# Decay matrices of a bidirectional state space layer: 512-column row matmuls and masks on the diagonal blocks only

## The chip, the cores and the metric

The kernel runs on one core of a Trainium2 chip. The time is the device time of one launch in microseconds (us), the median of several runs. Five engines work from instruction streams of their own: TensorE (PE, with its weight loads shown apart as PEld), VectorE (DVE), ScalarE (ACT), GpSimd (POOL) and SyncE (SP), which here issues the transfers. Matrix products land in PSUM, which has eight banks of 512 float32 columns on each of 128 partitions.

## What is computed

One layer of an encoder with 256 tokens and 1024 features: a gated feed-forward half step, a mixer that adds latent attention (16 heads) and a state space part (SSD), and a second half step. The change concerns the SSD part, which runs once forward and once backward over the tokens and has 32 heads in 4 groups of 8:

```
a_cs = cumsum(dt * a)                              # log decay up to each token
seg  = a_cs[l] - a_cs[s]
decay = exp(where(tril, seg, -inf))                # [l, s], per head
cb   = C @ B.T                                     # [l, s], per group
y    = (cb * decay) @ (x * dt)                     # plus the chunk states
y_total = y_forward + reverse(y_backward of reversed inputs)
```

The kernel does not scan chunks. It works on the full 256 x 256 matrix of token pairs, as 2 x 2 blocks of 128 x 128: the forward direction needs the two diagonal blocks (each a triangle) and one block beside them, the backward direction the two diagonal blocks (the other triangle) and the opposite one. Six blocks are needed for a head.

## The kernel before

Weights are float32. Each one that comes from memory is split by `wload` into a rounded part (`whi`, ScalarE, L94) and the rest (`wlo`, VectorE, L97), and every product with a weight is three matmuls of 256 columns in the type fp32r (`mm3`, L136 to L138). The first half step runs 22 blocks of such products and 8 for the way back; the second does the same at the end. Between them is the mixer.

In the mixer, `in_group` projects and convolves the inputs of one SSD group, `attn_group` does two attention heads, `ssd_group` one group of eight SSD heads as `start`, four times `pair`, and `finish`. These units, the gates' projections and half of the branch products are put into one list, `plan`, sorted by hand-set keys (`A0`, `DA`, `S0`, ...), and traced in that order. The build's scheduler then orders each engine's stream: it takes the ready instruction of the highest priority, where priority is the place in the trace, and where the splitting of weights is put ahead by 50 (`WPRI`). So matmuls of a projection may stand between those of a `pair`. Each engine then runs its stream in order.

For SSD, partition is the token `s` that gives and column the token `l` that takes. `tables` and the code from L463 prepare:

- `acs` [128, 2, 64], the sums of log decays, counted from the middle of the sequence outwards; `nacs` is its negative. Index 1 is the half of the sequence, index 2 the head (0 to 31 forward, 32 to 63 backward).
- `st1` and `st2` (L477 to L493), 256 columns each: the sums with heads on partitions and tokens on columns, as a rounded part and, on other partitions, a rest. `st1` holds forward and backward heads, `st2` for each half of the tokens the heads of the opposite direction.
- `sel1` and `sel2`, columns with a one at the partitions of a head. A column spread over 128 columns as the stationary operand gives a matmul that copies a head's row of `st1` or `st2` to all partitions.
- `msk`, three windows of `msk4` of 256 columns each: 0 where a pair of tokens counts and -2**100 elsewhere. With the identity `eye` as the stationary operand a matmul adds it.

`pair` takes two heads. It fills three PSUM banks `ps_pl` in turn, `i` = 0, 1, 2, each with 256 columns for either head: `i` = 0 is what the first half of the tokens gives going forward, `i` = 1 what the second half gives going backward, `i` = 2 the two diagonal blocks of the opposite directions. For each bank and head there is one matmul with the mask (L672) and one with the row (L673). ScalarE takes the exponential with `nacs` as bias (L678: 256 columns; L680 and L681: 128 each), VectorE multiplies the bank's 512 columns by `cb` (L683, shown as L97), and eight matmuls per pair (L690; float32, for which the profile shows two records each) sum the blocks into `ps_y`, in the order of the banks. There are two `ps_pl` buffers (`NPL`) and four `E` buffers (`EB`).

Of the kernel before, what the change touches and what calls it, by code (L numbers as in the profile page):

```python
# [8 lines left out]
F32 = mybir.dt.float32  # L9
F32R = mybir.dt.float32r  # L10
# [13 lines left out]
# pool depths  # L24
# [48 lines left out]
def build(ctx, tc, A, out, dbg=None):  # L73
# [131 lines left out]
    class Norm:  # L205
        """x * gain of each tile of x as it comes, and the sum of squares"""
# [159 lines left out]
    with ExitStack() as es:  # L366
# [63 lines left out]
        # rotated shared key and its square sum  # L430
# [12 lines left out]
        # dt = softplus(raw + bias), log-decay sums  # L443
# [22 lines left out]
        # log-decay sums counted from the middle of the sequence outwards  # L466
# [13 lines left out]
        for c in range(2):  # L480
            V.tensor_copy(dup[:, 0, c].rearrange("p (a b) -> p a b", a=2),
                          acs[:, c].unsqueeze(1).to_broadcast([P, 2, 64]))
            o = 32 * (1 - c)
            V.tensor_copy(dup[:, 1, c].rearrange("p (a b) -> p a b", a=4),
                          acs[:, c, o:o + 32].unsqueeze(1).to_broadcast([P, 4, 32]))
        pd = gbank("ps_dup")
        for i in range(2):
            for c in range(2):
                TE.transpose(pd[:, (2 * i + c) * P:(2 * i + c + 1) * P], dup[:, i, c], ident)
# [49 lines left out]
        def attn_group(g):  # L539
            st = {}  # L540

            def proj():
# [20 lines left out]
                # head norms  # L563
# [11 lines left out]
                # rotary part of q, in place  # L575
# [7 lines left out]
                # k  # L583
# [55 lines left out]
        def ssd_group(g, xz):  # L639
            st = {}  # L640

            def start():
# [6 lines left out]
                cb = (cb[:, 0:2], cb[:, 2:4], cb[:, 0:4:3])  # L649
                st["cb"] = cb  # L650
# [12 lines left out]
            def pair(p):  # L663
                cb = st["cb"]
                M = []
                for i in range(3):
                    pp = ps_pl.tile([P, 2, T], F32, tag="pl", name="ps_pl")
                    E = ss.tile([P, 2, T], F32, tag="E", name="E", bufs=EB)
                    for j in range(2):
                        h = 8 * g + 2 * p + j  # L670
                        lh = sel1[:, 32 * i + h:32 * i + h + 1] if i < 2 else sel2[:, h:h + 1]
                        TE.matmul(pp[:, j], eye, msk[i], start=True, stop=False)  # L672
                        TE.matmul(pp[:, j], lh.to_broadcast([P, P]), st1 if i < 2 else st2, start=False, stop=True)  # L673
                    for j in range(2):
                        h = 8 * g + 2 * p + j
                        if i < 2:
                            o = 32 * i + h
                            ends[1] = S.activation(E[:, j], pp[:, j], AF.Exp, bias=nacs[:, i, o:o + 1])  # L678
                        else:
                            S.activation(E[:, j, 0:P], pp[:, j, 0:P], AF.Exp, bias=nacs[:, 0, 32 + h:33 + h])  # L680
                            ends[1] = S.activation(E[:, j, P:T], pp[:, j, P:T], AF.Exp, bias=nacs[:, 1, h:h + 1])  # L681
                    E4 = E.rearrange("p j (a b) -> p j a b", a=2)
                    tt(E4, E4, cb[i].unsqueeze(1).to_broadcast([P, 2, 2, P]), ALU.mult)  # L683
                    M.append(E)
                py = gbank("ps_y")
                plan = ((0, 0, 0, 0, T), (1, 1, 1, 0, T), (0, 1, 2, 0, P), (1, 0, 2, P, T))
                for n, (c, d, i, a, b) in enumerate(plan):
                    for j in range(2):
                        hh_ = 2 * p + j
                        TE.matmul(py[64 * j:64 * j + 64, a:b], st[c, d][:, hh_], M[i][:, j, a:b],  # L690
                                  start=n == 0, stop=n == 3)
                y = st["y"][:, p]
                dc = V_DSK + 4 * g + p
                stt(y, xz[1 + p // 2][:, p % 2], vec[:, dc:dc + 1], py[:, :T], ALU.mult, ALU.add)
                tt(y, y, xz[3 + p // 2][:, p % 2], ALU.mult)

            def finish():
                y = st["y"]
                sq = [ss.tile([P, 2, T], F32, tag="E", name="ysq", bufs=EB) for _ in range(2)]
# [95 lines left out]
def _tiles(w):  # L795
    """[K, M] -> [M tiles, partition, K tiles, 128]"""
# [4 lines left out]
def _pairs(t):  # L801
    """[n, P, K, 128] -> [n / 2, P, 2 * K * 128]"""
# [89 lines left out]
```

## Time and profile before

| | us |
|---|---|
| median of 3 runs | 820.86 |
| lowest, highest | 820.34, 820.87 |
| profiled execution, from the first to the last instruction | 817.6 |
| PE idle in the span | 817.6 - 797.8 = 19.8 |

No other time is given for the profiled execution than its span; the median of the runs is 3.26 us above it.

The first half step lies at about 0 to 211 us, the mixer at 211 to 633, the second half step after that. The 16 calls of `pair` lie between 260.9 us, where the first matmul of `ps_pl` starts, and 555.4 us, where the last of `ps_y` does.

A matmul's length in the profile is its latency. Matmuls follow each other faster than that, so the distance from one start to the next says what one costs. In a row of a group the last part is the idle time of the engine just before these instructions, and what ended it; in a row of the timeline this stands in brackets.

### The profile page before, as it was taken

To read this page: it belongs to the slowest core of one execution; us is meant where nothing else is said; L and a number is where in the kernel's file an instruction comes from. 1 tells how busy PE (TensorE), PEld (TensorE's weight loads), DVE (VectorE), ACT (ScalarE), POOL (GpSimd) and SP (SyncE) were. 2 spreads that over 40 slices of the span, in tenths; PEclk is the share of its full clock that TensorE was granted. 3 is DMA by queue.
4 is the path that set the end of the run, shared out by engine and by line. 5 is a ranking of instruction groups with operands and counts; after the bars stand their busy time and mean duration, and the time that the engine had idled before them with its cause. 6 is when DMAs were issued, how large, how long until landed. Compare 5 with 4: busy or idle time off the path is not lost.

```text
span 817.6 us, 16082 instructions
## 1 busy us (share of the span) xinstructions
PE 797.8 (98%) x6480; PEld 768.8 (94%) x6480; DVE 590.3 (72%) x1192; ACT 470.2 (58%) x810; POOL 0.2 (0%) x4
## 2 busy tenths in 40 slices
PE   6999999999998999999999999999999999999998
PEld 5999999999998998988989999999999999999998
DVE  6977776566797986897897578657787766666543
ACT  6755554455367659679676666557455544444342
POOL 0000000000000000000000000000000000000000
PEclk9999999999999999999999999999999999999999
DMA  7667774667235443322325414342665555554772
GB/s 259 214 212 224 222 229 136 184 184 215 63 92 171 131 131 104 106 79 92 103 85 168 154 52 154 112 146 68 223 184 178 175 184 182 185 184 131 197 206 75
DMA packets 39098, 126.61 MB, mean 155 GB/s; under 512 B 4464, under 2 KB 5872, under 8 KB 39024
## 3 DMA queue, kind: packets, MB, share of 16 engines
q1 hardware_dynamic: 38592, 124.69, 48.7%
q8 instruction: 51, 0.84, 0.4%
q10 hardware_dynamic: 432, 0.89, 0.3%
q14 instruction: 23, 0.19, 0.1%
HBM read 124.52 MB, written 1.05 MB: 154 GB/s over the span
## 4 chain that ended last, share of the span: by engine, by line
PE 86%; DVE 6%; ACT 5%; DMA 2%; issue 1%; ACTq 0%
PE ps_gu L137 10%; PE ps_gu L138 10%; PE ps_gu L136 10%; PE ps_d L136 5%; PE ps_d L137 5%; PE ps_d L138 5%; PE ps_in L137 4%; PE ps_in L138 4%; PE ps_in L136 4%; PE ps_y L690 3%; PE ps_sb L138 2%; PE ps_sb L137 2%; PE ps_sb L136 2%; PE ps_sc L603 2%; PE ps_gt L137 1%; PE ps_o L630 1%
## 5 line engine op out<-in xcount | busy, mean ns | idle before, releaser
L94 ACT ACTIVATE whi<-raw 128x1024 fp32r<-128x1024 f32 (+4 forms) x256 | 251.3, 986 | 209.0 <-PE ps_d L137 53.1
L97 DVE TENSOR_TENSOR wlo<-raw,whi 128x1024 fp32r<-128x1024 f32 (+4 forms) x256 | 289.8, 1134 | 112.1 <-ACT whi L94 111.2
L136 PE MATMUL ps_gu<-xh,whi 128*128 128x256 f32 x704 | 201.0, 285 | 7.9 <-ACT whi L94 7.9
L137 PE MATMUL ps_gu<-xl,whi 128*128 128x256 f32 x704 | 201.2, 286 | 0.5 <-DVE xl L100 0.4
L138 PE MATMUL ps_gu<-xh,wlo 128*128 128x256 f32 x704 | 200.8, 285 | 0.0
L136 PEld LDWEIGHTS ps_gu<-xh,whi 128*128 128x128 f32 x704 | 136.5, 194 | 8.2 <-ACT whi L94 8.2
L137 PEld LDWEIGHTS ps_gu<-xl,whi 128*128 128x128 f32 x704 | 136.5, 194 | 1.0 <-DVE xl L100 0.9
L138 PEld LDWEIGHTS ps_gu<-xh,wlo 128*128 128x128 f32 x704 | 136.4, 194 | 0.5 <-DVE wlo L97 0.5
L137 PE MATMUL ps_in<-xl,whi 128*128 128x256 f32 x368 | 105.3, 286 | 0.1
L138 PE MATMUL ps_in<-xh,wlo 128*128 128x256 f32 x368 | 105.0, 285 | 0.0
L136 PE MATMUL ps_in<-xh,whi 128*128 128x256 f32 x368 | 104.4, 284 | 0.0
L137 PE MATMUL ps_d<-hl,whi 128*128 128x256 f32 x352 | 99.1, 281 | 0.0
L136 PE MATMUL ps_d<-hh,whi 128*128 128x256 f32 x352 | 99.1, 281 | 0.0
L138 PE MATMUL ps_d<-hh,wlo 128*128 128x256 f32 x352 | 99.0, 281 | 0.0
L137 PEld LDWEIGHTS ps_in<-xl,whi 128*128 128x128 f32 x368 | 70.1, 191 | 0.6 <-DVE xl L100 0.3
L138 PEld LDWEIGHTS ps_in<-xh,wlo 128*128 128x128 f32 x368 | 70.1, 191 | 0.5 <-issue 0.3
L136 PEld LDWEIGHTS ps_in<-xh,whi 128*128 128x128 f32 x368 | 70.1, 191 | 0.1
L136 PEld LDWEIGHTS ps_d<-hh,whi 128*128 128x128 f32 x352 | 66.3, 188 | 0.0
L137 PEld LDWEIGHTS ps_d<-hl,whi 128*128 128x128 f32 x352 | 66.3, 188 | 0.0
L138 PEld LDWEIGHTS ps_d<-hh,wlo 128*128 128x128 f32 x352 | 66.3, 188 | 0.0
L100 DVE SCALAR_TENSOR_TENSOR xz<-ps_in,vec,xz 128x254 f32<-128x254 f32 (+1 forms) x96 | 44.8, 476 | 1.6 <-ACT xz L520 0.9
L94 ACT ACTIVATE hh<-sg 128x256 fp32r<-128x256 f32 x44 | 18.1, 415 | 45.9 <-DVE sg L97 45.9
(222 smaller groups left out, 1467.5 us busy)
## 6 DMA issues: line engine op xcount, KB each, us to landing
raw<-in_w_gu SPq DMA_DIRECT2D x86, 512.0 KB, 4.5
raw<-in_w_in SPq DMA_DIRECT2D x62, 512.0 KB, 4.4
raw<-in_w_d SPq DMA_DIRECT2D x32, 384.0 KB, 3.2
raw<-in_w_d SPq DMA_DIRECT2D x32, 320.0 KB, 3.4
raw<-in_w_sb SPq DMA_DIRECT2D x16, 512.0 KB, 4.4
raw<-in_w_qkv SPq DMA_DIRECT2D x8, 544.0 KB, 3.8
raw<-in_w_ab SPq DMA_DIRECT2D x8, 512.0 KB, 3.8
raw<-in_w_o SPq DMA_DIRECT2D x8, 512.0 KB, 4.2
```

Source lines behind the costliest of these rows:

```text
L94: S.activation(dst, src, AF.Copy, scale=scale)
L97: V.tensor_tensor(out=dst, in0=a, in1=b, op=op)
L100: V.scalar_tensor_tensor(out=dst, in0=a, scalar=s, in1=b, op0=op0, op1=op1)
L136: TE.matmul(ps, whi, xhi, start=first, stop=False)
L137: TE.matmul(ps, whi, xlo, start=False, stop=False)
L138: TE.matmul(ps, wlo, xhi, start=False, stop=last)
L603: TE.matmul(sc[:, t * T:(t + 1) * T], qk[:HD, t * P:(t + 1) * P], qk[:HD, T:2 * T], start=True, stop=True)
L630: TE.matmul(po[64 * j:64 * j + 64, :T], kv[:, kt, HG * NOPE + hh_ * 64:HG * NOPE + (hh_ + 1) * 64], st[hh_][:, kt], start=kt == 0, stop=kt ...
L690: TE.matmul(py[64 * j:64 * j + 64, a:b], st[c, d][:, hh_], M[i][:, j, a:b], start=n == 0, stop=n == 3)
```

## The change

For each head one whole bank now holds forward (columns 0 to 255, given by the first half of the tokens) and backward (256 to 511, given by the second half). One matmul of 512 columns writes both rows from a wider `st1` [128, 2, 256], and one matmul of 256 columns adds the masks to the two diagonal blocks, columns 0 to 127 and 384 to 511; the other blocks get no mask. The third bank holds the opposite diagonal blocks of both heads: a matmul of 512 columns writes the masks (two blocks, repeated for the second head), two of 256 columns add the rows from `st2`. The exponentials keep their shapes and numbers. The product with `cb` on a head's bank is flat over 512 columns. `ps_y` takes the third bank first, then the two heads' banks. `sel1` and one mask block go; one `sel` of 32 columns serves forward and backward. The rest of the diff takes out comments.

```diff
-    sel1 = cp.tile([P, 64], F32R, name="sel1")
-    sel2 = cp.tile([P, 32], F32R, name="sel2")
+    sel = cp.tile([P, 32], F32R, name="sel")
     eye = cp.tile([P, P], F32R, name="eye")
-    msk4 = cp.tile([P, 4, P], F32R, name="msk4")
-    msk = (msk4[:, 2:4], msk4[:, 0:2], msk4[:, 1:3])
+    msk = cp.tile([P, 3, P], F32R, name="msk")
...
-        V.tensor_copy(sel1, cst[:, C_S1:C_S1 + 64])
-        V.tensor_copy(sel2, cst[:, C_S2:C_S2 + 32])
+        V.tensor_copy(sel, cst[:, C_S2:C_S2 + 32])
...
-        ts(msk4[:, 0], ones, 1.0, 2.0 ** 100, ALU.subtract, ALU.mult)
-        ts(msk4[:, 1], triB, 1.0, 2.0 ** 100, ALU.subtract, ALU.mult)
-        ts(msk4[:, 2], triF, 1.0, 2.0 ** 100, ALU.subtract, ALU.mult)
-        ts(msk4[:, 3], ones, 1.0, 2.0 ** 100, ALU.subtract, ALU.mult)
+        for i, tri in enumerate((triF, triB, triF)):
+            ts(msk[:, i], tri, 1.0, 2.0 ** 100, ALU.subtract, ALU.mult)
...
-        st1 = mp.tile([P, T], F32R, name="st1")
-        st2 = mp.tile([P, T], F32R, name="st2")
+        st1 = mp.tile([P, 2, T], F32R, name="st1")
+        st2 = mp.tile([P, 2, P], F32R, name="st2")
...
-        copy(st1, pd[:, 0:T])
-        tt(st1[64:128], pd[64:128, 0:T], st1[64:128], ALU.subtract)
-        copy(st2, pd[:, T:2 * T])
-        tt(st2[32:64], pd[32:64, T:2 * T], st2[32:64], ALU.subtract)
+        pd = pd.rearrange("p (a b) -> p a b", a=2)
+        copy(st1, pd)
+        tt(st1[32:64], pd[32:64], st1[32:64], ALU.subtract)
+        V.tensor_copy(st2[:, 0], st1[:, 1, 0:P].bitcast(F32))
+        V.tensor_copy(st2[:, 1], st1[:, 0, P:T].bitcast(F32))
...
             def pair(p):
                 cb = st["cb"]
+                h0 = 8 * g + 2 * p
+
+                def line(h):
+                    return sel[:, h:h + 1].to_broadcast([P, P])
+
+                def bank():
+                    return ps_pl.tile([P, 2, T], F32, tag="pl", name="ps_pl")
+
+                def decays(E, pieces, c):
+                    for a, b, src, k, o in pieces:
+                        ends[1] = S.activation(E[:, a:b], src, AF.Exp, bias=nacs[:, k, o:o + 1])
+                    tt(E, E, c, ALU.mult)
+
                 M = []
-                for i in range(3):
-                    pp = ps_pl.tile([P, 2, T], F32, tag="pl", name="ps_pl")
-                    E = ss.tile([P, 2, T], F32, tag="E", name="E", bufs=EB)
+                for j in range(2):
+                    h = h0 + j
+                    pp = bank()
+                    TE.matmul(pp, line(h), st1, start=True, stop=False)
+                    TE.matmul(pp.rearrange("p a (b c) -> p (a b) c", b=2)[:, 0:4:3], eye, msk[:, 0:2], start=False, stop=True)
+                    E = ss.tile([P, 2 * T], F32, tag="E", name="E", bufs=EB)
+                    decays(E, ((0, T, pp[:, 0], 0, h), (T, 2 * T, pp[:, 1], 1, 32 + h)), cb)
+                    M.append(E)
+
+                pp = bank()
+                TE.matmul(pp.rearrange("p a (b c) -> p a b c", b=2), eye,
+                          msk[:, 1:3].unsqueeze(1).to_broadcast([P, 2, 2, P]), start=True, stop=False)
+                for j in range(2):
+                    TE.matmul(pp[:, j], line(h0 + j), st2, start=False, stop=j == 1)
+                E = ss.tile([P, 2 * T], F32, tag="E", name="E", bufs=EB)
+                E4 = E.rearrange("p (a b) -> p a b", a=4)
                 for j in range(2):
+                    for c in range(2):
+                        o = 32 * (1 - c) + h0 + j
+                        ends[1] = S.activation(E4[:, 2 * j + c], pp[:, j, c * P:(c + 1) * P], AF.Exp, bias=nacs[:, c, o:o + 1])
+                E5 = E.rearrange("p (j c k) -> p j c k", j=2, c=2)
+                tt(E5, E5, cb.rearrange("p (a b) -> p a b", a=4)[:, 0:4:3].unsqueeze(1).to_broadcast([P, 2, 2, P]), ALU.mult)
...
-                plan = ((0, 0, 0, 0, T), (1, 1, 1, 0, T), (0, 1, 2, 0, P), (1, 0, 2, P, T))
-                for n, (c, d, i, a, b) in enumerate(plan):
+                plan = ((0, 1, 0, P), (1, 0, P, T), (0, 0, 0, T), (1, 1, 0, T))
+                for n, (c, d, a, b) in enumerate(plan):
                     for j in range(2):
-                        hh_ = 2 * p + j
-                        TE.matmul(py[64 * j:64 * j + 64, a:b], st[c, d][:, hh_], M[i][:, j, a:b],
+                        m = E[:, j * T + a:j * T + b] if n < 2 else M[j][:, c * T:(c + 1) * T]
+                        TE.matmul(py[64 * j:64 * j + 64, a:b], st[c, d][:, 2 * p + j], m,
                                   start=n == 0, stop=n == 3)
```

More of the change, by code (lines that the diff above doesn't have):

```diff
@@ L476, in build @@
         ts(nacs, acs, -1.0, None, ALU.mult)
-        st1 = mp.tile([P, T], F32R, name="st1")
-        st2 = mp.tile([P, T], F32R, name="st2")
+        st1 = mp.tile([P, 2, T], F32R, name="st1")
+        st2 = mp.tile([P, 2, P], F32R, name="st2")
         dup = m0.tile([P, 2, 2, P], F32, name="dup")
[L480 to L485, printed above, removed]
+        for d in range(2):
+            for c in range(2):
+                V.tensor_copy(dup[:, d, c].rearrange("p (a b) -> p a b", a=4),
+                              acs[:, c, 32 * d:32 * d + 32].unsqueeze(1).to_broadcast([P, 4, 32]))
         pd = gbank("ps_dup")
-        for i in range(2):
+        for d in range(2):
             for c in range(2):
-                TE.transpose(pd[:, (2 * i + c) * P:(2 * i + c + 1) * P], dup[:, i, c], ident)
-        copy(st1, pd[:, 0:T])
-        tt(st1[64:128], pd[64:128, 0:T], st1[64:128], ALU.subtract)
-        copy(st2, pd[:, T:2 * T])
-        tt(st2[32:64], pd[32:64, T:2 * T], st2[32:64], ALU.subtract)
+                TE.transpose(pd[:, (2 * d + c) * P:(2 * d + c + 1) * P], dup[:, d, c], ident)
+        pd = pd.rearrange("p (a b) -> p a b", a=2)
[3 more added lines that the diff above has]
+        V.tensor_copy(st2[:, 1], st1[:, 0, P:T].bitcast(F32))
         dump("acs", acs)
@@ L648, in start @@
                 copy(cb, pc.rearrange("p (a b) -> p a b", a=4))
-                cb = (cb[:, 0:2], cb[:, 2:4], cb[:, 0:4:3])
-                st["cb"] = cb
+                st["cb"] = cb.rearrange("p a b -> p (a b)")
                 for c in range(2):
@@ L664, in pair @@
                 cb = st["cb"]
-                M = []
-                for i in range(3):
-                    pp = ps_pl.tile([P, 2, T], F32, tag="pl", name="ps_pl")
-                    E = ss.tile([P, 2, T], F32, tag="E", name="E", bufs=EB)
-                    for j in range(2):
[L670 to L684, printed above, removed]
@@ L685, in pair @@
-                py = gbank("ps_y")
-                plan = ((0, 0, 0, 0, T), (1, 1, 1, 0, T), (0, 1, 2, 0, P), (1, 0, 2, P, T))
-                for n, (c, d, i, a, b) in enumerate(plan):
-                    for j in range(2):
-                        hh_ = 2 * p + j
-                        TE.matmul(py[64 * j:64 * j + 64, a:b], st[c, d][:, hh_], M[i][:, j, a:b],
+                h0 = 8 * g + 2 * p
+                def line(h):
+                    return sel[:, h:h + 1].to_broadcast([P, P])
@@ new lines, in pair @@
+                pp = bank()
[5 more added lines that the diff above has]
+                E4 = E.rearrange("p (a b) -> p a b", a=4)
+                for j in range(2):
+                    for c in range(2):
+                        o = 32 * (1 - c) + h0 + j
+                        ends[1] = S.activation(E4[:, 2 * j + c], pp[:, j, c * P:(c + 1) * P], AF.Exp, bias=nacs[:, c, o:o + 1])
@@ new lines, in pair @@
+                E5 = E.rearrange("p (j c k) -> p j c k", j=2, c=2)
+                tt(E5, E5, cb.rearrange("p (a b) -> p a b", a=4)[:, 0:4:3].unsqueeze(1).to_broadcast([P, 2, 2, P]), ALU.mult)
+                py = gbank("ps_y")
+                plan = ((0, 1, 0, P), (1, 0, P, T), (0, 0, 0, T), (1, 1, 0, T))
+                for n, (c, d, a, b) in enumerate(plan):
+                    for j in range(2):
+                        m = E[:, j * T + a:j * T + b] if n < 2 else M[j][:, c * T:(c + 1) * T]
+                        TE.matmul(py[64 * j:64 * j + 64, a:b], st[c, d][:, 2 * p + j], m,
@@ L698, in finish @@
                 y = st["y"]
-                sq = [ss.tile([P, 2, T], F32, tag="E", name="ysq", bufs=EB) for _ in range(2)]
+                sq = [ss.tile([P, 2 * T], F32, tag="E", name="ysq", bufs=EB).rearrange("p (a b) -> p a b", a=2) for _ in range(2)]
                 for i in range(2):
```

## The prediction

> **What bounds the kernel now.** The page's head, its busy line and its clock row come first, then the chain that ended last.
>
> ```profile
> span 817.6 us, 16082 instructions
> PE 797.8 (98%) x6480; PEld 768.8 (94%) x6480; DVE 590.3 (72%) x1192; ACT 470.2 (58%) x810; POOL 0.2 (0%) x4
> PEclk9999999999999999999999999999999999999999
> PE 86%; DVE 6%; ACT 5%; DMA 2%; issue 1%; ACTq 0%
> ```
>
> TensorE is busy in 98% of the span at full granted clock and carries 86% of the chain that ended last. A microsecond taken from its stream is a microsecond of time wherever it has other work ready, and nothing where something else paces it. So the next view is busy time by stage, in stretches of 10 us of the mixer (columns: length, PE, PEld, DVE, ACT, POOL busy, clock, DMA share, GB/s).
>
> ```profile
> 240.00:250.00 10.00, 10.00 (x86) 10.00 (x86) 9.70 (x21) 5.56 (x8) 0.00 (x0) 1.00 0.57 169
> 300.00:310.00 10.00, 10.00 (x87) 10.00 (x86) 6.65 (x17) 6.29 (x8) 0.00 (x0) 1.00 0.67 215
> 310.00:320.00 10.00, 8.90 (x69) 7.24 (x68) 4.31 (x10) 9.97 (x22) 0.00 (x0) 1.00 0.14 49
> 380.00:390.00 10.00, 8.91 (x72) 7.62 (x71) 8.05 (x16) 10.00 (x28) 0.00 (x0) 1.00 0.22 68
> 540.00:550.00 10.00, 10.00 (x77) 8.10 (x76) 6.27 (x10) 5.79 (x14) 0.00 (x0) 1.00 0.43 140
> ```
>
> Most stretches look like the first two and the last: PE at 10.00. In 310:320 and 380:390 ScalarE is full and PE has a gap; there a saving on PE may turn into a wait.
>
> **The change part by part.** The code that changes most is the decay part of `pair`, run 16 times. The groups by line and shape, and one undisturbed run of its matmuls in the timeline (columns: start, length, engine and line):
>
> ```profile
> L672 PE MATMUL ps_pl<-msk,eye 128*128 128x256 f32 x96 | 27.2, 310 | 2.2 <-ACT E L678 2.2
> L673 PE MATMUL ps_pl<-st,sel 128*128 128x256 f32 x96 | 24.6, 283 | 0.0
> L97 DVE TENSOR_TENSOR E<-E,cb 128x512 f32<-128x512 f32 x48 | 32.1, 686 | 1.8 <-ACT E L681 1.4
> 541.53 0.28 PE L672 MATMUL ps_pl<-msk,eye 128*128 128x256 f32 x1
> ...
> 542.35 0.28 PE L673 MATMUL ps_pl<-st,sel 128*128 128x256 f32 x1
> ```
>
> The means of 283 and 310 ns are latencies that overlap; what a matmul costs is the distance between starts. Eight of them begin from 541.53 to 542.35: 0.82 / 7 = 0.117 us each. Each pair has 12 such matmuls of 256 columns (192 / 16): 12 x 0.117 = 1.404 us.
>
> After the change a pair has 7: two rows of 512 columns into a head's whole bank, two masks of 256 columns on its diagonal blocks, one mask of 512 columns for the shared bank and two rows of 256 columns. That is 2560 columns in place of 3072. No matmul of 512 columns stands in the trace, so its price has to be bounded. Rows that show how cost follows width:
>
> ```profile
> 459.01 0.27 PE L597 MATMUL ps_qkT<-cst,qs 128*96 128x128 f32 x1
> ...
> 459.33 0.27 PE L598 MATMUL ps_qkT<-cst,ka 128*96 128x128 f32 x1
> 317.29 1.08 PE L690 MATMUL ps_y<-E,xd 128*64 128x256 f32 x8
> 318.31 0.31 PE L597 MATMUL ps_qkT<-cst,qs 128*96 128x128 f32 x1
> 318.55 0.66 PE L690 MATMUL ps_y<-E,xd 128*64 128x128 f32 x8
> 319.14 0.31 PE L598 MATMUL ps_qkT<-cst,ka 128*96 128x128 f32 x1
> ```
>
> Four transposes of 128 columns begin 0.32 / 3 = 0.107 apart, hardly less than the 0.117 of 256: at 128 columns something other than width, most likely the weight load, sets the distance. The `ps_y` records load only 64 weight columns and do follow width: eight of 256 columns take 318.31 - 317.29 = 1.02, or 0.1275 each, eight of 128 take 319.14 - 318.55 = 0.59, or 0.074 each; the difference is 0.0535 / 128 = 0.42 ns a column. A matmul of 512 columns is then 0.117 + 256 x 0.42 ns = 0.224 us. Its ends: 512 x 0.42 = 0.214 if nothing but width counts, and 2 x 0.117 = 0.234 if it costs as two. I take 0.224, which starts from the same kind of matmul.
>
> By the Trainium skill, page "TensorE: Matmul & The Clock Gate", section "LDWEIGHTS (loading the stationary operand)", a load of 128 columns takes 128 / 1.2 = 107 ns, which is the distance of the transposes above. That page's section "Back-to-back issue gap" also gives a sustained 131 ns for a matmul of 512 columns in a stream with weight loads, against about 216 for an isolated one; the 0.42 ns a column of `ps_y` agrees with the second figure and not with the first.
>
> A pair then costs 4 x 0.117 + 3 x 0.224 = 1.140 us, which saves 0.264, and 16 pairs save **4.2 us** (3.7 with 0.234, 4.7 with 0.214). Weight loads fall from 12 to 7 and stay beside matmuls.
>
> Not moved: the exponentials (four of 256 and four of 128 columns a pair, before and after) and three products of 512 columns on VectorE; their operand is flat now, and I give nothing for it: `gu` on VectorE with a broadcast operand and the plain `ysq` sum, both 128x512, show 689 and 687 ns.
>
> ```profile
> L97 DVE TENSOR_TENSOR gu<-ps_gu,R 128x512 f32<-128x512 f32 x44 | 30.2, 689 | 17.2 <-PE ps_gu L138 17.2
> L97 DVE TENSOR_TENSOR ysq<-ysq 128x512 f32<-128x512 f32 x4 | 2.7, 687 | 1.2 <-ACT ysq L701 1.2
> ```
>
> Set-up: `sel1` and one mask operation go, the copy and subtraction for `st1` become twice as wide, `st2` becomes two copies of 128 columns. These are tenths of a microsecond, once each, under matmuls of the first half step and of stretch 240:250, where PE is at 10.00; I cost them at nothing. Uncovered they would be about 0.5 us. No DMA is added or moved, and SP's queue stays as it is.
>
> **What is given back.** Two places. First, where ScalarE paces:
>
> ```profile
> 316.42 0.38 PE L672 MATMUL ps_pl<-msk,eye 128*128 128x256 f32 x1 [1.08 <-ACT E L678]
> 381.61 0.39 PE L672 MATMUL ps_pl<-msk,eye 128*128 128x256 f32 x1 [1.09 <-ACT E L678]
> ```
>
> Both wait for the exponential that frees one of the two `ps_pl` banks. What PE saves just ahead of them, one bank's worth, is waited out: 0.2 us each, 0.4 together.
>
> Second, the `ps_y` matmuls take the shared bank first, so all eight wait for the pair's third product; before, the first four needed the first two products only. Products on VectorE, and the `ps_y` that ran before the third one ended:
>
> ```profile
> 316.76 1.36 DVE L97 TENSOR_TENSOR E<-E,cb 128x512 f32<-128x512 f32 x2
> 381.96 1.36 DVE L97 TENSOR_TENSOR E<-E,cb 128x512 f32<-128x512 f32 x2
> 382.49 1.08 PE L690 MATMUL ps_y<-E,xd 128*64 128x256 f32 x8
> 465.79 1.08 PE L690 MATMUL ps_y<-E,xd 128*64 128x256 f32 x8
> 466.80 0.69 DVE L97 TENSOR_TENSOR E<-E,cb 128x512 f32<-128x512 f32 x1 [0.83 <-ACT E L681]
> 544.84 0.65 PE L690 MATMUL ps_y<-E,xd 128*64 128x256 f32 x4
> 545.89 0.69 DVE L97 TENSOR_TENSOR E<-E,cb 128x512 f32<-128x512 f32 x1 [0.55 <-ACT E L681]
> 552.02 1.36 DVE L97 TENSOR_TENSOR E<-E,cb 128x512 f32<-128x512 f32 x2
> 553.02 0.59 PE L690 MATMUL ps_y<-E,xd 128*64 128x256 f32 x2
> ```
>
> In five pairs `ps_y` began before the third product ended: 316.76 + 1.36 = 318.12 against 317.29, 0.83 us early; likewise 0.83 at 382, 1.7 at 466, 1.7 at 545 and 0.36 at 553. In the other eleven it starts after all three. At 466, 545 and 553 gate and branch matmuls lie beside and can go first. At 317 and 382 what stands behind `ps_y` on PE are the next head's transposes and the next pair's `ps_pl`, about 0.9 us that can be issued ahead; if it is not, they wait too, and so do `yg` on VectorE and, through the four `E` buffers, the next exponentials. Between nothing and 0.83 I take 0.4 at these two and nothing at the others: 0.8. Sum: 4.2 - 0.4 - 0.8 = **3.0 us**.
>
> The profiled execution spans 817.6 us and would span 814.6. The runs have a median of 820.86, 3.26 above that span, for what lies around it; nothing in the change touches that. Forecast: 820.86 - 3.0 = **817.9 us**.
>
> **Rivals.**
> 1. *The wide matmul is far cheaper.* If a matmul of 512 columns cost 0.131, a pair would be 4 x 0.117 + 3 x 0.131 = 0.861, saving 0.543 x 16 = 8.7, less 1.2: 813.4. The figure is the Trainium skill's 131 ns named above. Against it stand the `ps_y` rows; 4%.
> 2. *The saving is waited out.* The build's scheduler places instructions by priority and readiness; with fewer ahead of them, the exponentials and weight splits may pace more stretches as in 310:320 and 380:390, and PE's gaps grow by what its work shrinks. Then about 820.9, give or take 1. For it: ScalarE or VectorE stands over 9 in three of the five stretches quoted. Against it: PE is at 10.00 in 540:550, which holds the run of `ps_pl` quoted above, with gate and branch matmuls between; 16%.
> 3. *Slower: `ps_y` waits for the third product in most pairs.* From the second product to the third lie four exponentials at about 0.25 us and a product of 0.686, 1.7 us, of which 0.83 was unhidden at 317. The change breaks even when the mean unfilled wait of a pair reaches 4.2 / 16 = 0.26 us. With 0.83 in eight pairs, 6.6 - 4.2 + 0.4 = 2.8 us slower: 823.7. Against it: eleven pairs now start `ps_y` after all products; 8%.
> 4. *Slower: the mask on diagonal blocks is slow.* It writes columns 0 to 127 and 384 to 511 of a bank, with a hole; no matmul here does that. A far row for a slow one of 256 columns is the score matmul:
>
> ```profile
> 312.44 1.13 PE L603 MATMUL ps_sc<-qk 96*128 96x256 f32 x4
> 313.22 0.47 PE L136 MATMUL ps_in<-xh,whi 128*128 128x256 f32 x1
> ```
>
> Four records, two to a matmul, take 0.78: 0.39 a matmul. At that price 32 masks cost 32 x (0.39 - 0.117) = 8.7 more: 817.9 + 8.7 = 826.6. The Trainium skill, page "PSUM — Partial Sum Buffer", section "Specifications (TRN2)", says that any non-contiguous access pattern slows matmuls significantly, which speaks against this change; no run here shows it yet. For the change: runs of 128 neighbouring columns are as long as a transpose's whole output, and those keep 0.107; 4%.
>
> **How the numbers follow.** The forecast has 68%, by its own terms 816 to 819.2 (price of the wide matmul 3.7 to 4.7, given back 0 to 2.1, which is 0.4 and 0.83 at two pairs). About 0.2%, 1.64 us, is what a measurement can tell from no change. Faster: forecast and rival 1, 72%. Same: rival 2, 16%. Slower: rivals 3 and 4, 12%. The range of 815.6 to 821.6 takes in the forecast with its bounds and nearly all of rival 2.
>
> **What would show it.** Right: `ps_pl` has 112 matmuls in place of 192; a row of 512 columns is followed by the next start after about 0.224 us; a diagonal mask after 0.117; PE's idle ahead of `ps_pl` and `ps_y` grows by no more than about a microsecond. Wrong: starts after a diagonal mask nearer 0.39 (rival 4), 0.131 behind a wide one (rival 1), idle ahead of `ps_y` that ends with a product of `E` in most pairs (rival 3), or new gaps that end with ScalarE (rival 2). The forecast is wrong above all if the new order of the instructions, which I can't see, moves other waits by more than it saves.

## The result and the profile after

| | us |
|---|---|
| changed kernel, median of 5 runs | 824.46 (822.35 to 826.21) |
| kernel before, 5 runs | 820.87 (820.34 to 822.58) |
| ratio | 1.0056, 95% interval 1.0043 to 1.0069 |
| span of the profiled execution, before and after | 817.6 and 820.6 |

The changed kernel is slower by 0.56%. The forecast of 817.9 has the wrong sign, and the time lies above the range's end of 821.6. Of all runs reported below, one (of e16, 2685.76 us) was far slower than the rest, and its ratio leaves it out. The page of the changed kernel, its head, busy line and chain:

```profile
span 820.6 us, 15947 instructions
PE 795.6 (97%) x6400; PEld 760.9 (93%) x6400; DVE 589.5 (72%) x1191; ACT 470.6 (57%) x809; POOL 0.2 (0%) x4
PE 85%; DVE 8%; ACT 5%; DMA 1%; issue 1%; ACTq 0%
```

80 matmuls are gone and PE has 2.2 us less busy time, but the span is 3.0 us longer: PE idles 25.0 us of it where it idled 19.8. The chain's shares differ by a point or two from those of before. The price of the new matmuls is seen in an undisturbed place of the timeline after the change (start, length, engine, line):

```profile
267.88 0.39 PE L678 MATMUL ps_pl<-st,sel 128*128 128x512 f32 x1
268.11 0.28 PE L679 MATMUL ps_pl<-msk,eye 128*128 128x256 f32 x1
268.23 0.39 PE L678 MATMUL ps_pl<-st,sel 128*128 128x512 f32 x1
268.46 0.28 PE L679 MATMUL ps_pl<-msk,eye 128*128 128x256 f32 x1
268.58 0.28 PE L136 MATMUL ps_in<-xh,whi 128*128 128x256 f32 x1
```

From start to start a wide row takes 268.11 - 267.88 = 0.23 us and a diagonal mask 268.23 - 268.11 = 0.12. Summed over all `ps_pl` records, from each start to the next start and without the idle time in brackets, `ps_pl` holds PE for 26.2 us before and 22.6 after. The saving is there: 3.6 us. What took it back is idle time, found in the timeline of PE over 250 to 570. Before, beside the two rows at 316.42 and 381.61 that the prediction shows, the gaps of 0.5 us or more are these four:

```profile
257.30 0.70 PE L646 MATMUL ps_cb<-xz 128*128 128x256 f32 x2 [0.88 <-ACT xz L532]
259.96 0.66 PE L654 MATMUL ps_xT<-cst,xz 128*128 128x128 f32 x4 [1.53 <-ACT kv L94]
...
359.69 0.44 PE L620 MATMUL ps_pT<-cst,pr 128*128 128x128 f32 x2 [0.75 <-DVE pr L104]
...
424.87 0.44 PE L620 MATMUL ps_pT<-cst,pr 128*128 128x128 f32 x2 [0.51 <-DVE pr L104]
```

After, all of 0.5 us or more, with what PE does at the third pair of the second group in full:

```profile
259.07 0.66 PE L649 MATMUL ps_xT<-cst,xz 128*128 128x128 f32 x4 [1.52 <-ACT kv L94]
...
315.23 0.44 PE L616 MATMUL ps_pT<-cst,pr 128*128 128x128 f32 x2 [1.11 <-DVE pr L104]
...
317.07 0.50 PE L678 MATMUL ps_pl<-st,sel 128*128 128x512 f32 x1 [0.82 <-ACT E L694]
...
349.42 0.38 PE L138 MATMUL ps_in<-xh,wlo 128*128 128x256 f32 x1 [1.33 <-DVE wlo L97]
...
381.69 0.44 PE L616 MATMUL ps_pT<-cst,pr 128*128 128x128 f32 x2 [1.27 <-DVE pr L104]
381.88 0.48 PE L678 MATMUL ps_pl<-st,sel 128*128 128x512 f32 x1
382.20 0.38 PE L616 MATMUL ps_pT<-cst,pr 128*128 128x128 f32 x2
382.34 0.36 PE L679 MATMUL ps_pl<-msk,eye 128*128 128x256 f32 x1
383.53 0.52 PE L678 MATMUL ps_pl<-st,sel 128*128 128x512 f32 x1 [0.83 <-ACT E L694]
383.87 0.39 PE L679 MATMUL ps_pl<-msk,eye 128*128 128x256 f32 x1
384.26 2.83 PE L702 MATMUL ps_y<-E,xd 128*64 128x128 f32 x16
387.02 0.43 PE L593 MATMUL ps_qkT<-cst,qs 128*96 128x128 f32 x1
...
417.31 0.38 PE L138 MATMUL ps_in<-xh,wlo 128*128 128x256 f32 x1 [1.34 <-DVE wlo L97]
...
555.72 0.41 PE L616 MATMUL ps_pT<-cst,pr 128*128 128x128 f32 x2 [1.52 <-DVE pr L104]
```

Six gaps of 5.84 us in all have become eight of 9.74; with the smaller ones, from 0.15 us up, 6.81 has become 11.51, that is 4.7 more. Of the 3.9 us between 5.84 and 9.74, the two places that the prediction named give 1.9 (1.11 + 0.82 + 1.27 + 0.83 in place of 1.08 + 1.09). New waits at 349, 417 and 555 give 4.2, and the waits of before at 257, 359 and 424, 2.1 together, are gone or under 0.5 us.

At 381 one sees the named kind. Both banks of the *next* pair (L678, L679, twice) stand ahead of this pair's `ps_y`, and the second of them waits 0.83 us for the exponential that frees its bank. That wait is not what holds `ps_y`, though. VectorE makes the pair's third product at

```profile
383.51 0.69 DVE L97 TENSOR_TENSOR E<-E,cb 128x512 f32<-128x512 f32 x1 [1.00 <-ACT E L694]
```

which ends at 383.51 + 0.69 = 384.20, and `ps_y`, which now needs it first, starts 0.06 us later. So PE stands idle for want of the third product, and the next pair's banks fill a part of that time. At 555 it is the other way round: the pair's third product is ready early, but `ps_y` stands in PE's stream behind transposes that wait 1.52 us for `pr`:

```profile
552.94 0.68 DVE L97 TENSOR_TENSOR E<-E,cb 128x512 f32<-128x512 f32 x1
557.01 1.09 PE L702 MATMUL ps_y<-E,xd 128*64 128x128 f32 x12
```

Before, this `ps_y` ran from 553.02 on.

Back at 384, `ps_y` takes 387.02 - 384.26 = 2.76 us for 16 records. The windows of 2 us of the changed kernel say why (clock third from the end):

```profile
382.00:384.00 2.00, 1.17 (x8) 0.72 (x6) 1.00 (x2) 1.94 (x7) 0.00 (x0) 0.97 0.00 0
384.00:386.00 2.00, 2.00 (x14) 1.39 (x14) 1.71 (x3) 1.72 (x4) 0.00 (x0) 0.50 0.00 0
386.00:388.00 2.00, 2.00 (x13) 1.17 (x10) 1.27 (x3) 1.41 (x3) 0.00 (x0) 0.68 0.32 55
388.00:390.00 2.00, 2.00 (x15) 1.85 (x14) 1.73 (x4) 2.00 (x7) 0.00 (x0) 1.00 0.56 207
```

The granted clock was 0.50 for two microseconds and low on both sides: 2 x (0.03 + 0.50 + 0.32) = 1.7 us of clock. Before, the same four windows stand at 1.00. The account of the profiled execution is then -3.6 + 4.7 + 1.7 = 2.8 of the 3.0 us that the span grew.

### The profile page after: what moved, and what is told of

It reads as the page before. It is cut to its first block, busy times and chain, and to the rows that moved or that the text cites. A ratio compares the mean times of both kernels' runs of the same rounds, so it can differ in the third digit from the quotient of the medians.

```text
span 820.6 us, 15947 instructions
## 1 busy us (share of the span) xinstructions
PE 795.6 (97%) x6400; PEld 760.9 (93%) x6400; DVE 589.5 (72%) x1191; ACT 470.6 (57%) x809; POOL 0.2 (0%) x4
## 4 chain that ended last, share of the span: by engine, by line
PE 85%; DVE 8%; ACT 5%; DMA 1%; issue 1%; ACTq 0%
PE ps_gu L137 10%; PE ps_gu L138 10%; PE ps_gu L136 10%; PE ps_d L137 5%; PE ps_d L136 5%; PE ps_d L138 5%; PE ps_in L138 4%; PE ps_in L137 3%; PE ps_in L136 3%; PE ps_y L702 3%; PE ps_sb L138 2%; PE ps_sb L137 2%; PE ps_sb L136 2%; PE ps_gt L138 2%; PE ps_gt L137 2%; PE ps_gt L136 2%
```

## The experiments

The theories that were set against each other:

- **A**, the order of `ps_y`: taking the shared bank first puts `ps_y` behind the third product and the next pair's banks.
- **B**, the new layout of the banks, wide rows and masks with a hole, costs something itself.
- **C**, the draw: any edit makes the scheduler order all streams anew, and the new order happens to be a worse one.
- **D**, the clock that drops after the new gaps; **W**, the saving is waited out, because PE's work doesn't set the time.

All ratios are against the kernel before on the same chip.

**e1: the changed kernel, with `ps_y` in the order of before.**

```diff
-                plan = ((0, 1, 0, P), (1, 0, P, T), (0, 0, 0, T), (1, 1, 0, T))
+                plan = ((0, 0, 0, T), (1, 1, 0, T), (0, 1, 0, P), (1, 0, P, T))
...
-                        m = E[:, j * T + a:j * T + b] if n < 2 else M[j][:, c * T:(c + 1) * T]
+                        m = E[:, j * T + a:j * T + b] if n > 1 else M[j][:, c * T:(c + 1) * T]
```

> The changed kernel with ps_y taking the two heads' banks first and the shared bank last, as before the change. Theory A (the loss comes from ps_y waiting for the pair's third product, so that the next pair's bank is placed ahead of it on PE and PE stands still behind that bank's wait): the stalls of 0.82 and 0.83 us ahead of ps_pl and the clock drop at 382 to 388 go, and the saving of 4.2 us shows: 816.2 to 819. Theory B (the banks' new shape, a head's bank being ready only when both directions are in, starves ScalarE whatever the order of ps_y): stays at 823 to 826. Theory C (any new order of the streams gives a time of its own): anywhere from 817 to 826.

Measured: 818.83, ratio 0.9993 (0.9984 to 1.0001). The order of `ps_y` alone takes 0.63% away. Its timeline at the same pair:

```profile
380.55 0.44 PE L616 MATMUL ps_pT<-cst,pr 128*128 128x128 f32 x2 [1.29 <-DVE pr L104]
380.92 0.65 PE L702 MATMUL ps_y<-E,xd 128*64 128x256 f32 x2
381.49 0.44 PE L616 MATMUL ps_pT<-cst,pr 128*128 128x128 f32 x2
381.86 1.08 PE L702 MATMUL ps_y<-E,xd 128*64 128x256 f32 x6
...
383.26 0.48 PE L678 MATMUL ps_pl<-st,sel 128*128 128x512 f32 x1
383.68 0.66 PE L702 MATMUL ps_y<-E,xd 128*64 128x128 f32 x8
384.26 0.38 PE L679 MATMUL ps_pl<-msk,eye 128*128 128x256 f32 x1
384.49 0.39 PE L678 MATMUL ps_pl<-st,sel 128*128 128x512 f32 x1
```

The products of the heads fill the time in which the shared bank is made, the gap of 0.83 ahead of L678 is gone, and the last eight `ps_y` records need 384.26 - 383.68 = 0.58 us at full clock. More changed than this place. The gap at 349.42 of the changed kernel waits for a piece of a weight, `wlo`. VectorE there, in the changed kernel:

```profile
346.55 1.23 DVE L97 TENSOR_TENSOR ml<-yg,mh 128x1024 fp32r<-128x1024 f32 x1
...
348.16 1.21 DVE L97 TENSOR_TENSOR wlo<-raw,whi 128x1024 fp32r<-128x1024 f32 x1
```

and in e1:

```profile
345.97 1.22 DVE L97 TENSOR_TENSOR wlo<-raw,whi 128x1024 fp32r<-128x1024 f32 x1
347.23 1.23 DVE L97 TENSOR_TENSOR ml<-yg,mh 128x1024 fp32r<-128x1024 f32 x1
```

The scheduler put `ml` ahead of `wlo` in the one and behind it in the other. Nothing of the change touches either instruction, and it costs PE 1.33 us there and 1.34 at 417.31.

**e2: the kernel before, with the changed order of `ps_y`.**

```diff
-                plan = ((0, 0, 0, 0, T), (1, 1, 1, 0, T), (0, 1, 2, 0, P), (1, 0, 2, P, T))
+                plan = ((0, 1, 2, 0, P), (1, 0, 2, P, T), (0, 0, 0, 0, T), (1, 1, 1, 0, T))
```

> The kernel before with one change, the order of ps_y: shared bank first, the two others behind it. Matmul work as before. Theory A: it loses about what the changed kernel lost against its sum, 824.5 - (820.9 - 4.2) = 7.8 us, so 825 to 829, with gaps ahead of ps_pl and ps_y in the two ScalarE-paced stretches and possibly a clock below 1. Theory B: 820.9 within 1. Theory C: anywhere from 818 to 829.

Measured: 820.6, ratio 1.0012 (1.0001 to 1.0023). The order of `ps_y` alone costs about 1 us here, not the 5 of the changed kernel; A had 825 to 829.

**e3: the changed kernel with the shared bank made first.** The code of the third bank moves ahead of the loop over the two heads; `ps_y` still takes it first.

```diff
+                pp = bank()
+                TE.matmul(pp.rearrange("p a (b c) -> p a b c", b=2), eye,
+                          msk[:, 1:3].unsqueeze(1).to_broadcast([P, 2, 2, P]), start=True, stop=False)
...
                 M = []
                 for j in range(2):
                     h = h0 + j
```

> The changed kernel with the shared bank computed first as well, so that ps_y keeps the changed order but finds its operands in the order in which they are made. Theory A: as good as heads first, 816.2 to 819. Theory B: 823 to 826. Theory C: anywhere from 817 to 826.

Measured: 817.92, ratio 0.9981 (0.9971 to 0.9991): 0.75% below the changed kernel, with the same matmuls and the same order of `ps_y`. In this draw the cost seems to lie not in which bank `ps_y` takes first but in its taking first the one made last; moving the code also draws the order anew.

**e4: the kernel before with `WPRI` 45 in place of 50.** Nothing but the priority of the weight splits.

> The kernel before with the splitting of weights put ahead by 45 places in the trace in place of 50; nothing else. It measures what a small shift of the order alone does. Theories A and B: within 1.5 us of 820.9. Theory C: several us off, to either side.

Measured: 821.98, ratio 1.003 (1.0018 to 1.0042). An edit that changes no instruction costs 2.4 us. This is what theory C needs.

**e5: the changed kernel again, unaltered.**

> The changed kernel unaltered, on one chip with the next three, to read each run's granted clock beside its time. Theory D (most of the loss is the TensorE clock, halved for some microseconds behind the two stretches in which ps_y waits behind the next pair's bank): the runs line up on about 1.6 us of time for each 0.002 of mean clock (0.002 x 820), no run or hardly one has clock 1.000, and read back to clock 1.000 the kernel stands within 1.5 us of the kernel before. Against it: runs at clock 1.000 that are 3 us or more above the kernel before.

Measured: 823.72, ratio 1.0049 (1.0036 to 1.0063). The loss is repeatable. None of its six runs had a mean clock of 1.000; they lie at 0.996 to 0.998. This gives an estimate for D. The mean of the six is 0.9968, that of the kernel before in the same session 0.9993; 0.0025 x 820 = 2.0 us, so the clock is about half of the loss of 4.1 and the rest is not. The mean clock does not tell where a run lost it.

**e6 and e7: more work for PE.** The kernel before (e6) and e1 (e7) with the mask of the third bank added twice, which leaves the result as it is; e6 by the line below, e7 by the same matmul of 512 columns.

```diff
+                        if i == 2:
+                            TE.matmul(pp[:, j], eye, msk[i], start=False, stop=False)
```

> The kernel before with the shared bank's mask added twice (the result is the same): 32 matmuls of 256 columns more, 32 x 0.117 = 3.7 us of PE work, the mirror of what the change saves. If PE's work in the pairs sets the time (the prediction's premise): 3.7 us slower, plus or minus 1. If most of such work is waited out beside ScalarE and VectorE (theory W): slower by less than 1.5 us.

> The changed kernel with heads first and the shared bank's 512-column mask added twice: 16 x 0.23 = 3.7 us of PE work more than heads first, so about as much as the kernel before has. PE sets the time: 3.7 us over heads first, so near +0.4% against the kernel before. Theory W: within 1.5 us of heads first.

Measured: e6 825.29, ratio 1.0067 (1.0055 to 1.0079); e7 824.92, 1.0063 (1.005 to 1.0075). For 16 x 2 x 0.117 = 3.7 us of work e6 pays 0.67% or 5.5 us, and e7 0.70% over e1, both more than was expected. The times alone don't refute W, since e4 costs 2.4 us without any work. The profiles speak against it: `ps_pl` holds PE for 30.2 us in e6 where it was 26.2, and PE's idle time in the span is 823.5 - 802.6 = 20.9 us where it was 19.8. The added work did not go into idle time; how much of the 5.5 us the new order adds is not known.

**e8: the banks and the order of before, masks on the diagonal blocks only.** Per pair six rows and two masks of 256 columns and one mask of 512: as many columns as in the changed kernel, 2560.

```diff
+                    p4 = pp.rearrange("p j (c k) -> p j c k", c=2)
+                    if i == 2:
+                        TE.matmul(p4, eye, msk[2].unsqueeze(1).to_broadcast([P, 2, 2, P]), start=True, stop=False)
...
-                        TE.matmul(pp[:, j], eye, msk[i], start=True, stop=False)
-                        TE.matmul(pp[:, j], lh.to_broadcast([P, P]), st1 if i < 2 else st2, start=False, stop=True)
+                        TE.matmul(pp[:, j], lh.to_broadcast([P, P]), st1 if i < 2 else st2,
+                                  start=i < 2 and j == 0, stop=i == 2 and j == 1)
+                    if i < 2:
+                        TE.matmul(p4[:, :, i], eye, msk[i][:, i].unsqueeze(1).to_broadcast([P, 2, P]), start=False, stop=True)
```

> The kernel before with its own banks and its own order of ps_y; only the masks change: one matmul of 256 columns masks the diagonal blocks of both heads in the first and in the second bank, one of 512 columns masks the shared bank. 9 matmuls and 2560 columns a pair, 9 x about 0.13 = 1.16 us, as in the change. Theory B (the new banks cost what the matmuls save) and the prediction's premise: the saving shows, 3 to 4 us faster than before, -0.35 to -0.5%. Theory W: about as heads first, 0 to -0.2%.

Measured: 817.62, ratio 0.9974 (0.9963 to 0.9985), the lowest ratio of all versions, though short of the 0.35 to 0.5% that was expected. The gain of the shorter masks doesn't need the new layout.

**e9: e8 with the shared bank first in `ps_y`**, the fourth corner of layout against order.

> The kernel of e8 (the banks of before, masks on the diagonal blocks only) with the changed kernel's order of y: ps_y takes the shared bank first. It fills the fourth corner of layout against order of y. Theory A without any part for the layout (the order of y, once the masks are short, lets the next pair's bank slip ahead of y): 1.004 to 1.006 of before like the changed kernel, 823 to 824.5, with a granted clock under 1.000 and 4 us or more of added idle time on the matmul engine. If it needs the new layout as well: e8 plus about 1 us, as the order of y cost the kernel before, so 0.998 to 1.000 of before, at a clock of 1.000.

Measured: 821.63, ratio 1.0025 (1.0012 to 1.0038), between the two expectations; 0.51% above e8. With short masks the order of `ps_y` costs 0.5 to 0.6% in either layout, with the long ones of before 0.12%. B isn't needed. The three waits at 349, 417 and 555 of the changed kernel are in the timeline of e9 as well,

```profile
350.31 0.39 PE L138 MATMUL ps_in<-xh,wlo 128*128 128x256 f32 x1 [1.35 <-DVE wlo L97]
416.19 0.39 PE L138 MATMUL ps_in<-xh,wlo 128*128 128x256 f32 x1 [1.35 <-DVE wlo L97]
554.63 0.41 PE L620 MATMUL ps_pT<-cst,pr 128*128 128x128 f32 x2 [1.51 <-DVE pr L104]
```

and not one of them is in e1, e3 or e8; e2 has 0.89 us at 553.76. The profile of e9 has no wait of 0.83 us at a bank (near 317 and 382 it has 1.09 and 1.10 there, as e8 has 1.10 twice), and its clock is 1.000, yet it spans 819.3 us against the 815.3 of e8: with 1.35 + 1.35 + 1.51 = 4.2 us these three waits are enough for the whole difference. So in the order as given A's order of `ps_y` does the harm, but mostly by waits elsewhere and not by the one at the banks. By now A looked settled, for the scheduler's order as given. Whether it holds in other orders took the rest.

**e10 to e12: a second draw.** The kernel before, the changed one and e1, each with this edit:

```diff
-WPRI = 50
+WPRI = 70
```

> The kernel before with WPRI 70: nothing of the decays changed, only the planner's weight, so that the instructions come out in another order. It is the base for the next two. Lottery theory (C): a shift of 1 to 4 us to either side of before, as e4 gave with 45.

> The changed kernel with the same redrawn order. Theory A (the order of y is the cause): again 4 to 5 us above the next run, and a granted clock under 1.000. Theory C (the order that the planner happens to give is the cause): the difference to the next run changes size by more than 2 us or changes sign.

> e1 (the changed banks, heads planned first, y in the order of before) with the same redrawn order. Theory A: 4 to 5 us under the run ahead of it and within 1 us of the redrawn kernel before or below it. Theory C: anywhere within 4 us of the redrawn kernel before, without the gap to the run ahead of it.

**e13 to e16: a third draw.** The kernel before, the changed one, e1 and e8, with every state space unit a little later in the list:

```diff
-S0, DS, SF = 0.0193, 0.182, 0.896
+S0, DS, SF = 0.05, 0.182, 0.896
```

> The kernel before with S0 at 0.05 in place of 0.0193, so that every state space unit stands a little later in the list and the scheduler draws a third order. Base for the next three. From e4 and e10 (2.4 and 2.6 us above before): 820 to 825.

> The changed kernel in the third draw. Theory A (the order of y costs 2 to 5 us in every draw, the shorter masks give 2 to 3 back): within 2 us of the redrawn base above or below it, and 2 to 5 us above the next run. Theory C (the loss is the draw's): no such gap to the next run, less than 1 us or of the other sign.

> The changed banks with heads planned first, third draw. Theory A: 2 to 5 us under the run ahead of it and 0 to 3 us under the redrawn base. Theory C: anywhere within 4 us of the base.

> The banks and the order of y of before, masks on the diagonal blocks only (e8), third draw. If the shorter masks are a gain of their own: 1 to 3 us under the redrawn base, as e8 was 2.0 under before. If e8 was a lucky draw: level with the base or above it.

**e17 and e18: a fourth draw** of the kernel before and the changed one, with the attention units moved:

```diff
-A0, DA = -0.0991, 0.1594
+A0, DA = -0.07, 0.1594
```

> The kernel before with A0 at -0.07 in place of -0.0991, so that every attention unit stands a little later in the list: a fourth draw of the order, and the base of the next run. From the other draws of before (2.3 to 3.2 us above it): 820 to 823.

> The changed kernel in the fourth draw. If the loss is the change's own: 3 to 5 us above its redrawn base, as with the order as given. If the draw decides: anywhere from 4 us below that base to 4 us above it, more likely below or level, as in the second and third draw; a run with a clock of 1.000 lies some 0.8 us lower for each 0.001 of the clock than one without.

Measured, against the kernel before as given, and then each against the kernel before in its own draw (the quotient of the two ratios; the half-width is the root of the sum of squares of theirs):

| draw | before | changed | heads first | masks only | changed / before | heads first / before | masks only / before |
|---|---|---|---|---|---|---|---|
| as given | 1 | 1.0056 | 0.9993 | 0.9974 | 1.0056 ± 0.0013 | 0.9993 ± 0.0009 | 0.9974 ± 0.0011 |
| `WPRI` 70 | 1.0035 | 1.0033 | 1.0007 | | 0.9998 ± 0.0018 | 0.9972 ± 0.0015 | |
| `S0` 0.05 | 1.0039 | 0.9999 | 1.0009 | 1.0017 | 0.9960 ± 0.0019 | 0.9970 ± 0.0016 | 0.9978 ± 0.0016 |
| `A0` -0.07 | 1.0102 | 1.0082 | | | 0.9980 ± 0.0025 | | |

In us, from the second draw on: before 821.95, 822.87, 828.37; changed 821.38, 819.12, 827.11; heads first 819.37, 820.08; masks only 820.98.

Two things follow. First, A falls as a general cause: the changed kernel lies 0.63% above heads first as given and 0.26% in the second draw, but in the third it lies 0.10% below it. Second, against its own base the changed kernel is slower only in the order as given; in the others it is level, 0.40% faster, and 0.20% faster with an interval that reaches 1. The kernel before as given is the fastest of its five draws (e4 is the fifth), and the others are 0.3 to 1.0% behind it. A key moved by a little gave up that lead each time. An edit in `pair` need not: e1, e2, e3 and e8 were ordered anew too and lie from 0.26% below the base to 0.12% above it. Four draws with one key moved in each show that the order matters, not how often it goes one way.

The third draw is the clearest, because the same local pattern stands in its profile. The changed kernel there:

```profile
315.55 0.44 PE L616 MATMUL ps_pT<-cst,pr 128*128 128x128 f32 x2 [1.10 <-DVE pr L104]
...
317.39 0.49 PE L678 MATMUL ps_pl<-st,sel 128*128 128x512 f32 x1 [0.83 <-ACT E L694]
317.72 0.30 PE L679 MATMUL ps_pl<-msk,eye 128*128 128x256 f32 x1
318.12 2.83 PE L702 MATMUL ps_y<-E,xd 128*64 128x128 f32 x16
```

and the clock in its windows:

```profile
316.00:318.00 2.00, 1.17 (x6) 0.59 (x4) 0.99 (x2) 1.93 (x7) 0.00 (x0) 0.96 0.00 0
318.00:320.00 2.00, 1.91 (x15) 1.50 (x16) 1.71 (x3) 1.73 (x4) 0.00 (x0) 0.50 0.00 0
320.00:322.00 2.00, 2.00 (x14) 1.19 (x11) 1.28 (x4) 1.35 (x3) 0.00 (x0) 0.69 0.31 74
```

The next pair's banks are ahead of `ps_y` here too, with the same 0.83 us and the same drop of the clock, and yet the kernel beats its base. So this pattern alone doesn't make the change a loss. Nor does the drop belong to it: heads first in this draw (e15) has no wait at a bank there, only 1.10 us at 315.52, and its clock stands at 0.68 and 0.50 in the same first two windows. The order as given has the pattern twice, and the gaps at 349, 417 and 555 besides; no run takes these out one by one, but e9 shows that the latter three suffice for a loss. How much a draw can do shows the kernel before in the fourth, where one wait is larger than all that the change could save:

```profile
375.33 0.88 PE L620 MATMUL ps_pT<-cst,pr 128*128 128x128 f32 x3 [9.61 <-DVE pr L104]
```

With a base like that the fourth pair of runs says little by itself.

## Why the prediction was wrong

- **What bounds the kernel**: right as far as tested. e6 and e7 put work on PE and paid more than its length, and PE's idle time did not shrink.
- **The price of the matmuls**: right at the lower end. 0.224 us was taken for a wide row and 0.23 measured; the saving is 3.6 us by `ps_pl` in the changed kernel and 4.0 in e1 (22.2 in place of 26.2) where 4.2, with 3.7 to 4.7, was forecast. The first matmul of a bank after another kind costs some 0.1 us more than one in the stream: the wide mask at 379.69 starts 0.34 ahead of the next row at 380.03. In 37 of the 48 banks before and 36 after, the first matmul follows other work than `ps_pl`, so this hardly enters the difference.
- **Rival 1** (a wide matmul at 0.131): excluded by 0.23. **Rival 4** (a slow diagonal mask): excluded by 0.12. The Trainium skill, page "PSUM — Partial Sum Buffer", section "Specifications (TRN2)", warned of any non-contiguous access pattern; with blocks of 128 neighbouring columns the trace shows no cost.
- **Rival 2** (waited out): not so as a rule. e8 turns the same saving of columns into 0.26% of time, 0.22% in the third draw, and heads first saves 0.28 and 0.30% in two draws; as given it saves only 0.07%.
- **Rival 3** (`ps_y` waits for the third product in most pairs): not in most. It starts within 0.3 us of that product's end in four pairs of the changed kernel, at 317, 384, 470 and 548, and 1.5 us or more after it in the other twelve. At 317 and 384 the waiting is real, but it shows ahead of `ps_pl`, since the next pair's banks come in between. Its sign came true; its price, 0.83 in eight pairs, did not.
- **The step that failed is "What is given back", 1.2 us.** The wait for the third product at 317 and 382 was foreseen, and by idle time these two places cost 1.9 us, above the 1.2 taken and within its bound of 2.1. What the step put at nothing, without a reason, is every other place: it left out that the scheduler would order all the other instructions anew. New waits of 1.33, 1.34 and 1.52 us at 349, 417 and 555 outweigh the 2.1 us of waits that went. It also left out the clock, which fell at 382. In place of 1.2 us there stand 4.7 us of idle time and 1.7 of clock in the profiled execution. e9 against e8 shows the same three waits costing 4.0 us of span at a clock of 1.000.
- **The last sentence** of the prediction named this ("moves other waits by more than it saves") and gave it no chance and no price of its own. The runs give a price: the kernel before, drawn anew four times, moves by 2.4, 2.6, 3.2 and 8 us, each time up. That is of the size of the saving or above it.
- **3.26 us around the span** was too much: the runs of the changed kernel lie 1.8 above their own spans (822.35 against 820.6). The profiled execution of before was thus a quicker one than its median: 817.6 + 1.8 = 819.4, where later sessions have medians of 819.3 to 820.2 for it. This is an error of the base and not of the change.

The mechanism that was forecast exists: against its own base the change gives 0.9960 and 0.9980 in two of the three other draws (0.9998 in the third of them) and heads first 0.9972 and 0.9970, where 3.0 of 820.9 us is 0.9963. In the order as given it is covered by the waits that came with the new order of `ps_y`. How the loss divides between idle time and clock is known only roughly, half and half by the estimate at e5. The account by gaps above is not exact, as the busy lines of the changed kernel and of heads first in the second draw show, both profiled at a clock of 1.000:

```profile
PE 793.2 (97%) x6400; PEld 759.5 (93%) x6400; DVE 590.1 (72%) x1191; ACT 469.8 (57%) x809; POOL 0.2 (0%) x4
```

```profile
PE 797.0 (97%) x6400; PEld 763.4 (93%) x6400; DVE 590.0 (72%) x1191; ACT 470.3 (58%) x809; POOL 0.2 (0%) x4
```

The same 6400 matmuls count as 793.2 and 797.0 us busy, so some waiting hides in PE's busy time; the gaps of 0.15 us or more are 12.15 and 7.41 us, 4.7 apart, and the spans 819.4 and 817.6 only 1.8. Not settled either is why the scheduler's rule puts `ml` ahead of `wlo` in one kernel and behind it in the other.

## What to carry to other kernels

When a scheduler orders the streams, an edit is two changes: the one written and a new draw of the order. Here a key moved by a little, with no instruction changed, cost 2.4 to 8 us, as much as the edit could save. Measure an edit in several draws, each against its base in the same draw, before its own worth is judged, and then tune the keys again. In a chain of products, be wary of a sum that begins with the one made last: that order cost 0.63, 0.51, 0.26 and 0.12% in four comparisons here and nothing in a fifth, and in the order as given mostly by waits in other places than the sum.

## What the runs showed of the hardware

The granted clock of PE fell to 0.50 for some microseconds after gaps that were not long: 1.27 + 0.83 = 2.1 us idle within 4 us at 380 to 384 of the changed kernel, 1.10 + 0.83 in the third draw, and in the third draw of heads first a single gap of 1.10. The Trainium skill, page "TensorE: Matmul & The Clock Gate", section "Why this matters for your kernels", asks for no gaps over about 3 us; here shorter ones were enough. Nearly the same gaps at 315 to 317 of the changed kernel left the clock at 1.00, so it does not drop each time. It also drops where the change has no part: in the profile of the changed kernel in the third draw, whose mean clock is 0.996, it stands at 0.50 over 28 to 30 us too, in the first half step, after a gap of 1.34.

Runs of one kernel differ by it. The changed kernel of the third draw took 817.41 to 817.95 us in its four runs at a mean clock of 1.000, 818.69 to 820.29 in four at 0.998, 819.91 at 0.996, 821.27 and 823.41 at 0.994, and 823.04 at 0.992: a straight line through the twelve gives about 0.7 us for each 0.001.
